# First stage of a two-block model on one core: order of the loads, statistics by stream, place of the scale products

## The chip, the core and the metric

The kernel runs on one core of a Trainium2 chip. The metric is the device time of one execution in microseconds. The core has five engines that run side by side, each with its own queue of instructions: TensorE (PE, matrix products; PEld is its weight load), VectorE (DVE), ScalarE (ACT), GpSimd (POOL) and SyncE (SP, which here only issues transfers). Transfers run on 16 DMA engines.

## The reference, cut to what matters

Two transformer blocks in a row, for 256 tokens of width 1024. The change lies in the start of the first one, where the input x and a context ctx (256 tokens each) are normalised, scaled and shifted by vectors that come from a conditioning vector, and multiplied by the input weights of an mLSTM:

```python
mod = silu(c) @ w_mod + b_mod                 # 6 vectors of 1024: sh1, sc1, ga1, ...
mod_c = silu(c_ctx) @ w_mod + b_mod
hc = rmsnorm(ctx, g_mix) * (1 + csc1) + csh1  # the context stream
hx = rmsnorm(x, g_mix) * (1 + sc1) + sh1      # the latent stream
p = h @ w_in        # q, k, v, o and 16 gates of each token, for hx and hc
```

All that follows (the scan over chunks, the feed-forward parts, the second block) is unchanged.

## The kernel before, in words

The function `start` (lines 492 to 603) makes u = normalised input times scale plus shift for both streams, feature tile by feature tile (8 tiles f of 128 features), and at once multiplies it by the key and gate weights.

- **Loads.** SP issues, in the order of the trace: ccol (both conditioning vectors as columns), the identity, ctx in two pieces `xc` of 512 KB, x in two pieces of 512 KB, `wsc0` (the scale weights of tile 0, 512 KB, line 148), `cols` (all small column vectors, 211 KB), `wsh` of tile 0 (the shift weights, 512 KB, line 552), the key weights of tiles 0 to 3 (`raw`, 320 KB each, line 182), then scale and shift weights of tiles 1 to 4. POOL issues four loads at its start that are needed much later: `mpos` (128 KB, line 664), `row` (the head gain, 512 KB as a broadcast, line 400), `gout` (128 KB, line 1020) and `perm` (64 KB, line 1173).
- **Conditioning rows.** `cond_rows` (line 482) spreads the two conditioning vectors over all partitions with products against the identity.
- **Statistics.** For each of the four 128-token pieces, ScalarE sums the squares of the first 512 features (`mean_square`, line 324) and VectorE those of the other 512 (line 504). When all four are there, one series of ten small VectorE operations (line 507 and `rsqrt_half`, lines 298 to 317) gives the four reciprocal roots `r4`.
- **Features.** `features(h)` (line 510) scales half h of the features of both streams (`xn`, line 517 on VectorE, line 521 on ScalarE), transposes them on TensorE (line 528) and copies them to `xt` (line 530).
- **Vectors.** `vectors(f)` (line 545) makes the scale column of tile f by 8 products of `wsc` with the conditioning columns (`pg`, line 556; each is two hardware instructions, so 16 of them, with two columns each), read from PSUM by VectorE as `gsc` (line 563); and the shift column `shc` by two row sums of `wsh` on VectorE (`ttr`, line 256, 128x1024 each, and line 566). It also loads the key weights and splits them into a high part (a cast on ScalarE, line 236) and a low part (VectorE, line 237). All `pg` share one PSUM buffer (tag "tr" of a pool with one buffer).
- **Keys.** `keys(f)` (line 568) makes u on ScalarE (line 572), for tile 0 also a copy `u0` for wide products (line 576), splits u into high and low (`hilo`, lines 245 and 246), and issues 5 groups j of products into 5 PSUM buffers: per group of tiles 1 to 7 six products of 256 columns (lines 587 to 592), in tile 0 one of 512 columns (line 585) and four of 256.

The text of the program calls vectors(0), vectors(1), keys(0), features(1), and then vectors(f+1) and keys(f) in turn. That is not yet the order on an engine: a planner orders the instructions before the run, by priority (the order of the text; inside `urgent` they count as earlier), by when they are ready according to its own table of costs, and by free buffers. Each engine then works through its list strictly in order. `behind(op, first)` (line 187) adds an order between two instructions of an engine that the planner has to keep; it makes no wait. In `vectors`, for f from 3 on, the first scale product is put behind the key products of tile f-3 (line 558).

The functions that the change touches, as they stand:

Of the kernel before, what the change touches and what calls it, by code (L numbers as in the profile page):

```python
# [7 lines left out]
F32 = mybir.dt.float32  # L8
# [102 lines left out]
def kernel(ctx: ExitStack, tc: tile.TileContext, a: dict, out: bass.AP):  # L111
# [30 lines left out]
    wsc0 = hi_p.tile([128, 1024], F32, name="wsc", tag="w")  # L142
    xc = ar.tile([128, 2, D], F32, name="xc", tag="A")
# [4 lines left out]
    nc.sync.dma_start(out=wsc0, in_=a["w_sc"][0])  # L148

# [30 lines left out]
    def raw_load(src):  # L180
        r = raw_p.tile([128, 1024], F32, name="raw", tag="raw")
        nc.sync.dma_start(out=r[:, :src.shape[-1]], in_=src)
        return r
# [43 lines left out]
    def unit(src, slot=None):  # L227
        n = src.shape[-1]
        r = raw_load(src)
# [12 lines left out]
        return hi, lo  # L242
# [155 lines left out]
    def row_load(src):  # L398
        r = row_p.tile([128, D], F32, name="row", tag="row")
        G.dma_start(out=r[:, :src.shape[-1]], in_=src.partition_broadcast(128))  # L400
        return r
# [90 lines left out]
    def start():  # L492
# [4 lines left out]
        ss = sm.tile([128, 2, 4], F32, name="ss4", tag="ss4", bufs=1)  # L497
        cond_rows()
        for i, src in ((0, xc), (1, x)):
            for t in range(2):  # L500
                j = i * 2 + t
                mean_square(src[:, t, 0:512], ss[:, 0, j:j + 1], D)
                junk = wk.tile([128, D], BF16, name="gjunk", tag="gjunk", bufs=1)
                V.tensor_tensor_reduce(out=junk[:, 0:512], in0=src[:, t, 512:1024], in1=src[:, t, 512:1024], scale=0.5 / D,
                                       scalar=0.0, op0=ALU.mult, op1=ALU.add, accum_out=ss[:, 1, j:j + 1])
# [4 lines left out]
        def features(h):  # L510

            for i, src in ((0, xc), (1, x)):
                xn = wk.tile([128, 2, 512], F32, name="xn", tag="xn")
                for t in range(2):
                    w, r = src[:, t, h * 512:h * 512 + 512], r4[:, i * 2 + t:i * 2 + t + 1]
                    if t == 0:
                        o = V.tensor_scalar_mul(out=xn[:, t, :], in0=w, scalar1=r)
                        if h == 0:
                            mark["xn"] = mark["xn0"] = o
                    else:  # L520
                        o = S.activation(out=xn[:, t, :], in_=w, func=AF.Copy, scale=r)
                        if h == 0:
                            mark["xa"] = o
                for t in range(2):
                    pt = (acc_ps(i, t) if h == 0 else mm_ps() if t == 0 else
                          ps_tr.tile([128, 512], F32, name="pt", tag="tc")).rearrange("p (k n) -> p k n", k=4)
                    for k in range(4):
                        T.transpose(pt[:, k, :], xn[:, t, k * 128:k * 128 + 128], ident)
                    dst = xt[i][:, h * 4:h * 4 + 4, t * 128:t * 128 + 128]
                    (S.copy if t else V.tensor_copy)(dst, pt)  # L530

        with urgent():
            features(0)
# [6 lines left out]
        def kg_unit(f):  # L540
            if f < 1:
                pin(1, 4)
            kgu[f] = unit(a["a_kg"][f])

        def vectors(f):

            wsc = wsc0
            if f:
                wsc = hi_p.tile([128, 1024], F32, name="wsc", tag="w")
                nc.sync.dma_start(out=wsc, in_=a["w_sc"][f])  # L550
            wsh = lo_p.tile([128, 1024], F32, name="wsh", tag="w")
            nc.sync.dma_start(out=wsh, in_=a["w_sh"][f])
            kg_unit(f)
            pg = ps_tr.tile([128, 2], F32, name="pg", tag="tr")
            for k in range(8):
                o = T.matmul(pg, lhsT=wsc[:, k * 128:k * 128 + 128], rhs=ccol[:, k, :], start=(k == 0), stop=(k == 7))  # L556
                if k == 0 and f >= 3:
                    behind(o, mark["kg"][f - 3])
# [4 lines left out]
            o = V.tensor_scalar(out=gsc[:, f, :], in0=pg, scalar1=b1[:, f:f + 1], scalar2=col("g_mix", f, 1),  # L563
                                op0=ALU.add, op1=ALU.mult)
            behind(o, mark["xn"])
            V.tensor_scalar(out=shc[:, f, :], in0=shc[:, f, :], scalar1=col("b_mod", f, 1), scalar2=None, op0=ALU.add)

        def keys(f):
# [11 lines left out]
            hi, lo = kgu[f]  # L580
            for j in range(5):
                s = slice(j * 128, j * 128 + 128)
                p_ = kp[j] if j < 4 else gp
                if f == 0:
                    T.matmul(p_, lhsT=hi[:, s], rhs=u0, start=True, stop=False)
                else:
                    T.matmul(p_[:, 0:256], lhsT=hi[:, s], rhs=uc_hi[:, f, :], start=False, stop=False)
                    T.matmul(p_[:, 256:512], lhsT=hi[:, s], rhs=u_hi[:, f, :], start=False, stop=False)
# [4 lines left out]
            mark.setdefault("kg", []).append(o)  # L593

        vectors(0)
        vectors(1)
        for f in range(8):
            if 0 < f < 7:
                vectors(f + 1)
            keys(f)  # L600
            if f == 0:
                features(1)
# [4 lines left out]
    def mlstm():  # L607
# [56 lines left out]
        G.dma_start(out=mpos, in_=a["mpos"])  # L664
# [23 lines left out]
        gain = row_load(a["a_gain"])  # L688
# [320 lines left out]
    def gla():  # L1009
# [10 lines left out]
        G.dma_start(out=gout, in_=a["gl_gout"].partition_broadcast(128))  # L1020
# [132 lines left out]
    def rope_tables():  # L1153
# [19 lines left out]
        G.dma_start(out=mla.perm, in_=a["perm"])  # L1173
# [329 lines left out]
```

## Time and profile before

| | us |
|---|---|
| median of 3 runs | 1437.48 |
| the runs | 1437.48, 1437.93, 1434.57 |
| profiled execution, its own time | 1434.38 |
| its span | 1432.6 |
| TensorE busy in the span | 1380.0 (96%) |
| VectorE, ScalarE busy | 1113.9 (78%), 720.5 (50%) |
| mean share of the DMA engines' rate | 238 GB/s |

The span runs from the first to the last instruction of the profiled execution, the execution's own time is a little longer, and all rows below count microseconds from the start of the span. An engine that is busy most of the time over 1400 us says little on a stage of 70 us; for that, the views by windows, the chain of waits and the timelines are read. Matrix products are pipelined: the length of one in a row is longer than the distance between two starts, and the distance is what a product costs in a stream.

### The profile page before, as it was taken

What the parts mean: (1) busy time and instruction counts of PE and PEld (TensorE: products, weight loads), DVE (VectorE), ACT (ScalarE), POOL (GpSimd) and SP (SyncE); (2) the same over time, 40 slices, a digit from 0 to 9 for tenths busy, and PEclk for the clock granted to TensorE, in tenths of its full rate; (3) what the DMA queues carried; (4) which work ended last, traced back from release to release, by engine and by line L of the source; (5) the groups of instructions that cost most, each with busy time, mean ns of one, the idle gap of its engine ahead of it and who ended that gap; (6) DMA issues with size and microseconds to landing.
All of it is one profiled execution on the core that took longest, in us unless ns stands there. A gap on an engine that the chain in (4) does not pass through costs nothing.

```text
span 1432.6 us, 22526 instructions
## 1 busy us (share of the span) xinstructions
PE 1380.0 (96%) x8425; PEld 1204.0 (84%) x8425; DVE 1113.9 (78%) x2115; ACT 720.5 (50%) x1188; POOL 18.2 (1%) x42
## 2 busy tenths in 40 slices
PE   6999999999989999999999999999999999899997
PEld 6978877899978999878678999879999776789996
DVE  6887788898688888689788888698878786756563
ACT  4634764545354545566454545554554666644451
POOL 1000000000000000000000000000000000000000
PEclk8999999999999999999999999999999999999999
DMA  8576446797528999568548999469889472366750
GB/s 330 203 265 234 162 151 234 264 323 272 184 96 290 336 340 345 196 222 290 187 154 289 341 335 344 147 202 334 317 310 333 138 253 80 121 198 205 276 170 30
DMA packets 94943, 340.24 MB, mean 238 GB/s; under 512 B 10928, under 2 KB 11248, under 8 KB 94832
## 3 DMA queue, kind: packets, MB, share of 16 engines
q1 hardware_dynamic: 92736, 332.47, 65.6%
q0 software_dynamic: 2096, 6.33, 1.5%
q8 instruction: 66, 1.08, 0.3%
q14 instruction: 45, 0.37, 0.1%
HBM read 337.67 MB, written 1.08 MB: 236 GB/s over the span
## 4 chain that ended last, share of the span: by engine, by line
PE 70%; DVE 11%; DMA 10%; ACT 4%; issue 3%; SPq 0%; DVEq 0%; ACTq 0%; POOLq 0%
PE mm L250 12%; PE mm L252 11%; PE mm L251 11%; PE acc L252 8%; PE acc L250 8%; PE acc L251 8%; DMA raw<-in_cond_w_dram 3%; DVE wlo L237 3%; DVE gjunk L256 2%; PE acc L733 2%; ACT whi L236 1%; ACT ajunk L324 1%; PE pt L347 1%; PE pg L556 1%; DMA row<-d 1%
## 5 line engine op out<-in xcount | busy, mean ns | idle before, releaser
L237 DVE TENSOR_TENSOR wlo<-raw,whi 128x1024 fp32r<-128x1024 f32 (+1 forms) x385 | 462.5, 1207 | 109.6 <-ACT whi L236 106.7
L236 ACT CAST whi<-raw 128x1024 fp32r<-128x1024 f32 (+1 forms) x385 | 395.7, 1038 | 277.1 <-PE mm L251 79.5
L250 PE MATMUL mm<-u_hi,whi 128*128 128x256 f32 x1384 | 388.5, 281 | 0.2 <-DVE hf L831 0.2
L251 PE MATMUL mm<-u_lo,whi 128*128 128x256 f32 x1384 | 386.6, 279 | 0.0
L252 PE MATMUL mm<-u_hi,wlo 128*128 128x256 f32 x1384 | 386.5, 279 | 0.0
L250 PEld LDWEIGHTS mm<-u_hi,whi 128*128 128x128 f32 x1384 | 260.0, 188 | 4.4 <-DVE hf L831 0.6
L251 PEld LDWEIGHTS mm<-u_lo,whi 128*128 128x128 f32 x1384 | 259.3, 187 | 3.3
L252 PEld LDWEIGHTS mm<-u_hi,wlo 128*128 128x128 f32 x1384 | 260.1, 188 | 0.0
L256 DVE CUSTOM_DVE_ANT_0 gjunk<-raw,c 128x1024 bf16<-128x1024 f32 x192 | 234.3, 1221 | 24.1 <-DMA raw<-in_cond_w_dram 16.5
L250 PE MATMUL acc<-whi,hh 128*128 128x512 f32 x388 | 153.6, 398 | 4.5 <-ACT hh L245 4.5
L252 PE MATMUL acc<-whi,hl 128*128 128x512 f32 x388 | 153.3, 397 | 0.3 <-DVE hl L246 0.3
L251 PE MATMUL acc<-wlo,hh 128*128 128x512 f32 x388 | 152.5, 393 | 0.5 <-DVE wlo L237 0.5
L252 PEld LDWEIGHTS acc<-whi,hl 128*128 128x128 f32 x388 | 73.4, 189 | 17.4 <-DVE hl L246 0.7
L250 PEld LDWEIGHTS acc<-whi,hh 128*128 128x128 f32 x388 | 72.9, 188 | 17.5 <-ACT hh L245 5.0
L252 PE MATMUL acc<-whi,u_lo 128*128 128x512 f32 (+1 forms) x216 | 86.7, 403 | 0.5 <-DVE u_lo L246 0.5
L250 PE MATMUL acc<-whi,u_hi 128*128 128x512 f32 (+1 forms) x216 | 86.5, 401 | 0.0
L251 PE MATMUL acc<-wlo,u_hi 128*128 128x512 f32 (+1 forms) x216 | 86.4, 400 | 0.0
L251 PEld LDWEIGHTS acc<-wlo,hh 128*128 128x128 f32 x388 | 73.2, 189 | 14.2 <-DVE wlo L237 1.3
L251 PE MATMUL mm<-wlo,u_hi 128*128 128x512 f32 x144 | 57.3, 398 | 0.0
L250 PE MATMUL mm<-whi,u_hi 128*128 128x512 f32 x144 | 57.2, 397 | 0.0
L252 PE MATMUL mm<-whi,u_lo 128*128 128x512 f32 x144 | 57.0, 397 | 0.0
L946 ACT ACTIVATE sg<-mm 128x256 f32<-128x256 f32 x64 | 24.3, 380 | 59.6 <-PE mm L252 59.5
(734 smaller groups left out, 1998.6 us busy)
## 6 DMA issues: line engine op xcount, KB each, us to landing
raw<-in_cond_w_dram SPq DMA_DIRECT2D x144, 512.0 KB, 5.2
raw<-in_gu_ws_dram SPq DMA_DIRECT2D x128, 512.0 KB, 5.0
raw<-in_dn_dram SPq DMA_DIRECT2D x88, 512.0 KB, 4.9
raw<-in_gu_dram SPq DMA_DIRECT2D x48, 512.0 KB, 4.3
raw<-in_w_mod_dram SPq DMA_DIRECT2D x32, 512.0 KB, 4.3
raw<-in_f_down_dram SPq DMA_DIRECT2D x22, 512.0 KB, 4.6
raw<-in_f_gate_dram SPq DMA_DIRECT2D x18, 512.0 KB, 4.9
raw<-in_a_vo_dram SPq DMA_DIRECT2D x16, 512.0 KB, 5.1
```

Source lines behind the costliest of these rows:

```text
L236: o1 = S.copy(hi[:, :n], r[:, :n])
L237: o2 = V.tensor_tensor(out=lo[:, :n], in0=r[:, :n], in1=hi[:, :n].bitcast(F32), op=ALU.subtract)
L250: T.matmul(ps, lhsT=lh, rhs=rh, start=first, stop=False)
L251: T.matmul(ps, lhsT=lh, rhs=rl, start=False, stop=False)
L252: T.matmul(ps, lhsT=ll, rhs=rh, start=False, stop=last)
L256: return V.tensor_tensor_reduce(out=junk, in0=r, in1=vec, scale=1.0, scalar=0.0, op0=ALU.mult, op1=ALU.add, accum_out=dst)
L324: mark["ms"] = S.activation(out=junk[:, :src.shape[-1]], in_=src, func=AF.Square, scale=float(2 * width) ** -0.5, accum_out=dst)
L347: T.transpose(pt[:, k, :], src[:, (h * 4 + k) * 128:(h * 4 + k + 1) * 128], ident)
L556: o = T.matmul(pg, lhsT=wsc[:, k * 128:k * 128 + 128], rhs=ccol[:, k, :], start=(k == 0), stop=(k == 7))
L733: T.matmul(np_[:, 0:257], lhsT=w[:, d, s, :], rhs=vt[s][:, h, :], start=(i == 0), stop=(i == len(tiles) - 1))
L946: S.activation(out=sg, in_=ps[:, 0:256], func=AF.Silu)
```

## The change

What it does, part by part:

- `wsh0`, the shift weights of tile 0, is loaded right behind `wsc0`, ahead of `cols`.
- The other loads of the stage (key weights of tile 0, then scale, shift and key weights of tile 1, of tile 2 and so on) are issued by SP in one fixed order, each behind the one before (`load`).
- The four loads of POOL are issued by SP, behind the last of these (`late`).
- The statistics and roots are made for each stream by itself (`stats`), in the order ctx statistics, ctx features, x statistics, x features. Of x's first piece, ScalarE sums both halves; VectorE's sum of x's second piece is put behind the scaling of ctx.
- The scale products of tiles 0 and 1 stay in front. Those of tiles 2 to 7 are issued inside `keys(f)` for tile f+2: two products (four hardware instructions) behind each of the groups j = 0 to 3, and the first product of the next group is put behind them. `vectors(f+2)` is now called before `keys(f)`, where `vectors(f+1)` was.

Its core (left out: the loops around `features`, which now takes one stream, and two call sites of `late`):

```diff
+    wsh0 = lo_p.tile([128, 1024], F32, name="wsh", tag="w")
...
     nc.sync.dma_start(out=wsc0, in_=a["w_sc"][0])
+    nc.sync.dma_start(out=wsh0, in_=a["w_sh"][0])
...
+    def late(out, in_):
+        behind(nc.sync.dma_start(out=out, in_=in_), mark["loads"])
...
-        for i, src in ((0, xc), (1, x)):
+        def stats(i, src):
             for t in range(2):
                 j = i * 2 + t
                 mean_square(src[:, t, 0:512], ss[:, 0, j:j + 1], D)
+                if j == 2:
+                    mean_square(src[:, t, 512:1024], ss[:, 1, j:j + 1], D)
+                    continue
...
+                if i:
+                    behind(o, mark["xn0"])
+            js = slice(i * 2, i * 2 + 2)
+            V.scalar_tensor_tensor(out=ss[:, 0, js], in0=ss[:, 0, js], scalar=0.5 * EPS, in1=ss[:, 1, js], op0=ALU.add, op1=ALU.add)
+            r2.append(rsqrt_half(ss[:, 0, js], 2))
...
         with urgent():
-            V.scalar_tensor_tensor(out=ss[:, 0, :], in0=ss[:, 0, :], scalar=0.5 * EPS, in1=ss[:, 1, :], op0=ALU.add, op1=ALU.add)
-            r4 = rsqrt_half(ss[:, 0, :], 4)
...
+            for st in streams:
+                stats(*st)
+                features(0, *st)
...
+        def scales(f, k, after=None):
+            if k == 0:
+                pgs[f] = ps_tr.tile([128, 2], F32, name="pg", tag="tr")
+            pg = pgs[f]
+            o = T.matmul(pg, lhsT=wscs[f][:, k * 128:k * 128 + 128], rhs=ccol[:, k, :], start=(k == 0), stop=(k == 7))
+            mm = o
+            if after is not None:
+                behind(o, after)
+            if k == 7:
+                o = V.tensor_scalar(out=gsc[:, f, :], in0=pg, ...)
+                behind(o, mark["xn"])
+            return mm
+
+        def load(out, in_):
+            o = nc.sync.dma_start(out=out, in_=in_)
+            if "loads" in mark:
+                behind(o, mark["loads"])
+            mark["loads"] = o
...
             hi, lo = kgu[f]
+            turn = None
             for j in range(5):
...
+                if turn is not None:
+                    behind(o, turn)
...
                 o = T.matmul(p_[:, 256:512], lhsT=lo[:, s], rhs=u_hi[:, f, :], start=False, stop=f == 7)
-            mark.setdefault("kg", []).append(o)
+                if j < 4 and f < 6:
+                    for k in (j * 2, j * 2 + 1):
+                        turn = scales(f + 2, k, o)
...
-        vectors(0)
-        vectors(1)
+        for f in range(2):
+            vectors(f)
+            for k in range(8):
+                scales(f, k)
         for f in range(8):
-            if 0 < f < 7:
-                vectors(f + 1)
+            if f < 6:
+                vectors(f + 2)
             keys(f)
...
-        G.dma_start(out=mpos, in_=a["mpos"])
+        late(out=mpos, in_=a["mpos"])
```

## Rows read from the trace of the kernel before

**Rows 1.** Windows, 10 us long: busy time by engine, TensorE clock, DMA share, GB/s

```profile
40.00:50.00 10.00, 10.00 (x90) 10.00 (x88) 7.63 (x16) 3.91 (x9) 0.00 (x0) 1.00 0.58 204
```

**Rows 2.** Chain of waits, 0 to 110 us: start, length, what

```profile
3.85 10.56 DMA wsc<-in_w_sc_dram
...
14.55 3.55 PE pg L556 x16
...
18.10 3.28 PE acc L528 x16
...
21.41 0.59 ACT xt L530
...
23.71 1.09 ACT u L572 x2
...
25.67 0.79 PE acc L585
...
49.20 1.68 PE pg L556 x16
...
50.88 0.23 PE acc L587
...
52.73 1.01 PE pg L556 x10
...
53.74 0.22 PE acc L590
...
68.53 0.13 PE mm L592
```

**Rows 3.** DMA queues, 0 to 16 us: packets, MB, share of 16 engines' time

```profile
q1 hardware_dynamic: 1449, 3.80, 61.2%
...
q0 software_dynamic: 272, 0.85, 24.1%
```

**Rows 4.** Timeline of the SP queue: start, time to issue

```profile
5.54 6.66 SPq L182 DMA_DIRECT2D raw<-in_a_kg_dram  x4
...
13.14 0.33 SPq L550 DMA_DIRECT2D wsc<-in_w_sc_dram  x1
```

**Rows 5.** Timeline of VectorE and ScalarE, 8 to 24 us: start, length

```profile
8.78 0.63 ACT L324 ACTIVATE ajunk<-xc 128x512 bf16<-128x512 f32 x1 [2.04 <-DMA xc<-in_ctx_dram]
...
13.21 0.63 ACT L324 ACTIVATE ajunk<-x 128x512 bf16<-128x512 f32 x1 [0.55 <-DMA x<-in_x_dram]
...
14.08 0.17 DVE L507 SCALAR_TENSOR_TENSOR ss<-ss 128x4 f32<-128x4 f32 x1
...
16.66 0.48 DVE L517 TENSOR_SCALAR xn<-x,r 128x512 f32<-128x512 f32 x1
...
23.39 0.22 DVE L566 TENSOR_SCALAR shc<-shc,cols 128x2 f32<-128x2 f32 x1
```

**Rows 6.** Timeline of TensorE: start, length

```profile
31.78 0.60 PE L528 MATMUL mm<-ident,xn 128*128 128x128 f32 x4
...
53.80 0.28 PE L591 MATMUL acc<-v,wlo 128*128 128x256 f32 x1
...
55.33 0.28 PE L592 MATMUL mm<-u_hi,wlo 128*128 128x256 f32 x1
```

**Rows 7.** Windows before and in the first key products (columns as in rows 1)

```profile
21.50:23.50 2.00, 2.00 (x20) 1.96 (x18) 2.00 (x5) 2.00 (x4) 0.00 (x0) 1.00 1.03 410
...
28.00:31.00 3.00, 3.00 (x14) 2.81 (x14) 3.00 (x6) 0.62 (x2) 0.00 (x0) 0.50 1.01 385
```

**Rows 8.** Groups by shape, 0 to 75 us: busy, mean ns, idle before

```profile
L256 DVE CUSTOM_DVE_ANT_0 gjunk<-wsh,cc 128x1024 bf16<-128x1024 f32 x8 | 9.8, 1220 | 0.0
...
L237 DVE TENSOR_TENSOR wlo<-raw,whi 128x640 fp32r<-128x640 f32 x8 | 6.6, 821 | 0.0
...
L246 DVE TENSOR_TENSOR v<-u,v 128x256 fp32r<-128x256 f32 x8 | 3.4, 422 | 0.0
...
L563 DVE TENSOR_SCALAR gsc<-pg,b,cols 128x2 f32<-128x2 f32 x8 | 2.2, 277 | 6.5 <-PE pg L556 6.4
```

More of the change, by code (lines that the diff above doesn't have):

```diff
@@ L177, with raw_load @@
     mod2 = const.tile([128, 20, 8], F32, name="mod2")
-    def raw_load(src):
+    def raw_load(src, load=nc.sync.dma_start):
         r = raw_p.tile([128, 1024], F32, name="raw", tag="raw")
-        nc.sync.dma_start(out=r[:, :src.shape[-1]], in_=src)
+        load(out=r[:, :src.shape[-1]], in_=src)
         return r
@@ L506, in start @@
-        with urgent():
-            V.scalar_tensor_tensor(out=ss[:, 0, :], in0=ss[:, 0, :], scalar=0.5 * EPS, in1=ss[:, 1, :], op0=ALU.add, op1=ALU.add)
-            r4 = rsqrt_half(ss[:, 0, :], 4)
[L510 to L530, printed above, removed]
@@ L532, in start @@
-        with urgent():
-            features(0)
+                o = V.tensor_tensor_reduce(out=junk[:, 0:512], in0=src[:, t, 512:1024], in1=src[:, t, 512:1024],
+                                           scale=0.5 / D, scalar=0.0, op0=ALU.mult, op1=ALU.add, accum_out=ss[:, 1, j:j + 1])
+                if i:
+                    behind(o, mark["xn0"])
+            js = slice(i * 2, i * 2 + 2)
+            V.scalar_tensor_tensor(out=ss[:, 0, js], in0=ss[:, 0, js], scalar=0.5 * EPS, in1=ss[:, 1, js], op0=ALU.add, op1=ALU.add)
@@ new lines, in stats, with features @@
+            r2.append(rsqrt_half(ss[:, 0, js], 2))
+        def features(h, i, src):
+            xn = wk.tile([128, 2, 512], F32, name="xn", tag="xn")
+            for t in range(2):
+                w, r = src[:, t, h * 512:h * 512 + 512], r2[i][:, t:t + 1]
+                if t == 0:
+                    o = V.tensor_scalar_mul(out=xn[:, t, :], in0=w, scalar1=r)
+                    if h == 0:
+                        mark["xn"] = mark["xn0"] = o
+                else:
+                    o = S.activation(out=xn[:, t, :], in_=w, func=AF.Copy, scale=r)
+                    if h == 0:
+                        mark["xa"] = o
+            for t in range(2):
+                pt = (acc_ps(i, t) if h == 0 else mm_ps() if t == 0 else
+                      ps_tr.tile([128, 512], F32, name="pt", tag="tc")).rearrange("p (k n) -> p k n", k=4)
+                for k in range(4):
+                    T.transpose(pt[:, k, :], xn[:, t, k * 128:k * 128 + 128], ident)
+                dst = xt[i][:, h * 4:h * 4 + 4, t * 128:t * 128 + 128]
+                (S.copy if t else V.tensor_copy)(dst, pt)
@@ L538, in start, with vectors @@
         kgu = {}
-        def kg_unit(f):
+        wscs, pgs = {}, {}
+        def scales(f, k, after=None):
[7 more added lines that the diff above has]
+            if k == 7:
+                o = V.tensor_scalar(out=gsc[:, f, :], in0=pg, scalar1=b1[:, f:f + 1], scalar2=col("g_mix", f, 1),
+                                    op0=ALU.add, op1=ALU.mult)
+                behind(o, mark["xn"])
[5 more added lines that the diff above has]
+            mark["loads"] = o
+        def vectors(f):
+            wsc, wsh = wsc0, wsh0
+            if f:
+                wsc = hi_p.tile([128, 1024], F32, name="wsc", tag="w")
+                load(wsc, a["w_sc"][f])
+                wsh = lo_p.tile([128, 1024], F32, name="wsh", tag="w")
+                load(wsh, a["w_sh"][f])
             if f < 1:
                 pin(1, 4)
[L543 to L558, printed above, removed]
+            kgu[f] = unit(a["a_kg"][f], load=load)
             o = ttr(wsh, cc, shc[:, f, 0:1])
@@ L562, in vectors @@
             ttr(wsh, c1, shc[:, f, 1:2])
-            o = V.tensor_scalar(out=gsc[:, f, :], in0=pg, scalar1=b1[:, f:f + 1], scalar2=col("g_mix", f, 1),
-                                op0=ALU.add, op1=ALU.mult)
-            behind(o, mark["xn"])
+            wscs[f] = wsc
             V.tensor_scalar(out=shc[:, f, :], in0=shc[:, f, :], scalar1=col("b_mod", f, 1), scalar2=None, op0=ALU.add)
@@ L1019, in gla @@
         gout = hp.tile([128, 256], F32, name="gout", tag="gout", bufs=1)
-        G.dma_start(out=gout, in_=a["gl_gout"].partition_broadcast(128))
+        late(out=gout, in_=a["gl_gout"].partition_broadcast(128))
         units, got = {}, {}
@@ L1172, in rope_tables @@
         mla.perm = const.tile([128, 128], F32, name="perm")
-        G.dma_start(out=mla.perm, in_=a["perm"])
+        late(out=mla.perm, in_=a["perm"])
     def rope(src, dst, tokens, rp):
```

22 lines of the change are left out of this document (12 added, 10 removed).

## The prediction, made before the change was run

> **What bounds the kernel now.** The change touches the first stage only, so I read that stage, not the shares of the whole span. First the windows: what is to be seen is where TensorE has idle time and where its clock is full. From 40 to 50 us it is busy all the time at the full clock, while VectorE is busy for 7.6 and ScalarE for 3.9 of 10 us and DMA is at 0.58 [rows 1]. So once the key products run, TensorE's own work sets the pace, and waits of other engines there cost nothing. Second the chain of waits: its first link is the transfer of wsc0, which ends at 14.4; then come the scale products of tiles 0 and 1, transposes, the scaled features u at 23.71, the first key product at 25.67 and the last key product at 68.53 [rows 2]. So the stage has two parts: a front of 25.7 us that hangs on transfers and on a serial chain, and 42.9 us of TensorE's work. Time can be won by a shorter front, or by less work or fewer pauses behind it.
>
> **The loads.** Removed from the front are four transfers that POOL issued. In the first 16 us its queue moved 0.85 MB and took 24.1% of the time of the 16 DMA engines, 3.9 us; the other queue moved 3.80 MB in 61.2% of it, 9.8 us, by whose rate those bytes would take 2.2 us [rows 3]. These are the bounds for how much earlier x and wsc0 land; I take the middle, 3.1 us. The four transfers move to SP, behind the last key weights. They cost SP four issues of about 0.33 us each [rows 4], and the DMA engines 2.2 to 3.9 us around 45 us, where they are at 0.58 [rows 1]; what is queued behind them on SP are the query weights, which nobody waits for until the key products end. POOL loses four issues and had nothing waiting behind them. I cost all that at nothing; if the cover were gone, it would be those 2.2 to 3.9 us. The key weights of tiles 1 to 3 were issued at 5.5 to 12.2 us, ahead of the scale weights of tile 1 at 13.14 [rows 4]; now they alternate by tile. The bytes are the same. Tile 2's scale weights are now needed between the first key products; up to and with them, 5.7 MB are to be moved (the inputs and weights of 0.2 to 0.5 MB each in their new order), at 410 GB/s [rows 7] 13.8 us. Counted from 3.85, where wsc0 is issued [rows 2], that is 17.7, and at most a microsecond to land: ahead of 20.8 us, where I shall put the first key product. wsh0 moves in front of cols, 0.2 MB or 0.5 us; VectorE takes it up only behind x, so that is worth nothing by itself.
>
> **The statistics.** Before, the last piece of x is summed at 13.21, the joint series of small operations begins at 14.08 and x is scaled at 16.66 [rows 5]. The change adds a second series of ten small operations: from 14.08 to about 16.3, 2.2 us of VectorE. The first series (ctx) can run while x is landing: ctx's last piece was summed at 8.78 [rows 5], now 1 to 2 us earlier, so with 0.8 for the sum and 2.4 for the series ctx is scaled from about 10.5 to 11.0. x lands at 13.2 less 3.1, 10.1, but the VectorE half of its second piece now waits for the scaling of ctx: and behind it on that engine stands x's own series: sum from 11.0 to 11.8, series to 14.1, x scaled then, 2.6 us earlier than now. Moving one half of the first piece to ScalarE costs that engine 0.8 us while it waits for x: nothing.
>
> **To the first key product.** TensorE's work in between is 16 hardware products of the scale of tile 0, 3.55 us [rows 2] at half clock, and 16 transposes behind them, 3.28 us [rows 2]. Both ran one after the other; now they start at 11.0 with ctx's transposes, and 6.9 us of work end at 17.8. Then come the copy to xt (0.6), u (1.1) and the 0.87 from the end of u to the first product [rows 2], which gives 20.3, or 21.0 with one weight cast ahead of them. VectorE's side: from x scaled at 14.6 the two sums of wsh0 (2.6), a copy (0.7), a split (0.8), gsc and shc (0.5) [rows 5, 8] make 19.2, and with u and the rest 21.1. I take 20.8 for the first key product against 25.67: **4.9 us earlier**. The bounds are 22.5 to 23.5 (only the transfers shift, by 2.2 to 3.1) and 19.0 (sums slip into the gaps of the small series, transposes at the full clock): 2.2 to 6.7.
>
> **The scale products.** They are moved, not removed: 16 hardware products for each of tiles 2 to 7, 96 in all. Whether spreading them pays can be read from the trace, since the planner had already split one tile's. A block of 16 with the wide product behind it takes 1.68 and 0.23, less 0.118 for a wide one (13 of them from 53.80 to 55.33 [rows 6]): 1.79, or 0.112 each. A group of 10 takes 1.01 and 0.22, less 0.118: 1.11, or 0.111 each [rows 2]. So a split group costs what a block costs, and the edit is worth 0. The Trainium skill (TensorE: Matmul & The Clock Gate, Step-by-step: what each phase is for) says that TensorE pulls the next weight load ahead of a running product; by that, each of the four groups would hide one load more than the one block does, an estimated 3 x 0.112 x 6, 2.0 us less. The split group of 10 in this trace does not show it.
>
> VectorE waited 6.4 us for scale products [rows 8]; those waits go, but TensorE had no pause there [rows 1], so I count 0. What the change adds is order: the next group's first product follows each pair, so that a tile can no longer start with the products whose operands are ready; and one PSUM bank serves all scale products, so the first pair of a tile waits until VectorE has read the last tile's result (gsc). Between them lie 12 wide products, 1.4 us. What VectorE may have to finish first is between 0.3 (gsc alone) and 4.4 us (two sums, a split, two halves of u, gsc [rows 8]); so each of five tile changes costs between 0 and 3.0 us. VectorE's work per tile, 4.6 us, is less than TensorE's, 30 x 0.118 + 1.8 = 5.3, and gsc is due one whole tile ahead, so I take 0, the end that the pause-free rows are nearer to [rows 1].
>
> **The sum.** 4.9 us from the front, 0 behind it. The profiled run took 1434.4 us around a span of 1432.6; that gives 1429.5. The median of the three runs, 1437.5, stands 3.1 above it, one run beside it: by the median it would be 1432.6. I forecast **1431.0**, between the two.
>
> **The rivals.** *The clock stays up* (0.14, faster). The first 25 key products run from 25.67 [rows 2] to 31.78 [rows 6] and their clock is 0.50 [rows 7]; at the full clock 20 narrow ones at 0.118 and 5 of twice the columns at twice that would take 3.5: 2.6 us less. Just before, at 21.5 to 23.5, the clock was full [rows 7], and it fell in the pause in front of u. With TensorE at work from 11 us on it may be full when they start: 1431.0 - 2.6 = 1428.4. Against it: the scale products from 14.55 on took 3.55 us, 0.222 each where 0.112 is the full clock's price, so work of this kind had not raised it by 18 us. The Trainium skill (same page, What's actually happening) says that the clock is low by default and that sustained work releases it; by that rule this rival would be likelier than I make it.
>
> *The lead is lost* (0.22, within the bound). The strict order makes TensorE wait for the late halves of u in the first two tiles, while VectorE still has two tiles' sums in front of it. For it: VectorE gets tile 0's sums only at 14 us and has 4.6 us a tile. Against it: the slack of 0.7 us a tile. Price: 1 to 5 us; 1432 to 1436. That the order doesn't come out as written, since a planner places instructions, belongs here.
>
> *Slower* (0.08). The single PSUM bank: if VectorE's queue holds two sums and a split in front of gsc at each tile change, TensorE stands 5 times 3.0 us, 15 us, in place of a lead of 4.9: 1441. It decides from 1.0 us per tile (lead gone) and makes the kernel over 0.3% slower from 1.9. Against it: sums are spread between other work in VectorE's timeline, and the wait would have to come every time.
>
> *The loads don't land earlier* (0.04): if the queues only share the engines otherwise and x still lands at 13, the regrouping alone remains, about 1 us: 1435.
>
> **How the numbers follow.** About 0.3%, 4.3 us, is what a measurement of this kernel tells from no change. My forecast (0.52) lies at 4.9 between 2.2 and 6.7; about three quarters of it lie beyond 4.3 and count as faster, 0.39; with the clock's 0.14 that makes 0.53. Same: the other quarter, 0.13, the lost lead and the loads, together 0.39. Slower: 0.08. The range reaches from the front's upper bound with the clock, 1434.4 - 6.7 - 2.6, 1425, to 1437.5, where nothing is kept.
>
> **What would show it.** In the changed profile: x's sum at about 10 to 11 us in place of 13.2; the first key product at 19 to 22.5; the last at 62 to 65 in place of 68.5; no idle TensorE between; all pairs at 0.11 a product. It is wrong if TensorE shows pauses released by gsc or the halves of u, if x still lands at 13, or if the last key product is early and the end is not, which would mean that later transfers or VectorE give the lead back.

## The result, and the profile after

The changed kernel is **slower**: median 1444.59 us of 7 runs (1442.02 to 1452.67) against 1436.2 us of 7 runs of the kernel before (1432.32 to 1438.75); the ratio is 1.0069, 95% interval 1.0050 to 1.0088. The profiled execution took 1442.02 us with a span of 1439.8, 7.2 more than before. In the profiled executions all of it arises in the first 115 us:

| progress in the profiled executions, us | before | after | difference |
|---|---|---|---|
| x scaled | 16.66 | 14.23 | -2.4 |
| first key product | 25.67 | 22.77 | -2.9 |
| last key product | 68.37 | 72.66 | +4.3 |
| first value product | 68.49 | 77.95 | +9.5 |
| first score product of the attention | 102.16 | 113.81 | +11.6 |
| end of the span | 1432.6 | 1439.8 | +7.2 |

Some 4 us of the 11.6 come back near 1230 us, where the kernel before has a pause of 2.4 us and a clock of 0.66 over 10 us and the changed one has neither.

The front is as the change wanted it. The next fence is TensorE's timeline (start, length, then in brackets the idle time before and what ended it), with the last key product, the first value product and the first score product.

```profile
11.97 1.85 PE L563 MATMUL pg<-ccol,wsc 128*128 128x2 f32 x16
...
18.59 3.57 PE L563 MATMUL pg<-ccol,wsc 128*128 128x2 f32 x16 [1.23 <-DVE gsc L568]
22.02 1.09 PE L541 MATMUL pt<-ident,xn 128*128 128x128 f32 x4
22.77 0.78 PE L616 MATMUL acc<-u,whi 128*128 128x512 f32 x1
24.41 0.58 PE L623 MATMUL acc<-v,whi 128*128 128x256 f32 x1 [0.86 <-DVE v L248]
26.76 0.58 PE L624 MATMUL acc<-u_lo,whi 128*128 128x256 f32 x1 [1.76 <-DVE u_lo L248]
...
72.66 0.28 PE L626 MATMUL mm<-u_hi,wlo 128*128 128x256 f32 x1
77.95 1.22 PE L252 MATMUL acc<-whi,v 128*128 128x512 f32 x2 [5.01 <-ACT whi L238]
...
113.81 0.38 PE L745 MATMUL mm<-qT,kT 128*128 128x128 f32 x2
```

The scale products of tile 0 start at 11.97 in place of 14.55 [rows 2] and run at the full clock. But the block of tile 1, which before ran at the full clock while u was still being made, now waits 1.23 us for the scale of tile 0, takes 3.57 us at half clock and delays the first key product. Then tile 0 pauses twice for the late halves of u, 0.86 and 1.76 us. The largest pause is new and comes after the stage: 5.01 us in front of the first value product, ended by a ScalarE split of its weights. In the kernel before, the value products follow the last key product without a pause (its timeline of TensorE):

```profile
68.37 0.28 PE L592 MATMUL mm<-u_hi,wlo 128*128 128x256 f32 x1
68.49 0.63 PE L250 MATMUL acc<-whi,v 128*128 128x512 f32 x2
```

The windows show the clock (length, TensorE's busy time and count, granted clock, DMA share, GB/s), first of the kernel before, then of the changed one.

```profile
10.00:55.00 45.00, 38.32 (x280) 0.85 0.81 314
```

```profile
10.00:55.00 45.00, 39.36 (x250) 0.73 0.66 243
```

TensorE is busy a little longer in the changed kernel and gets 30 instructions less done. With two levels, 1.00 and 0.50, a mean of 0.85 over 45 us is 45 x 0.15 x 2 = 13.5 us at half clock, 0.73 is 24.3. The DMA share shows a second thing: 243 in place of 314 GB/s. The steady part answers to [rows 1]:

```profile
40.00:50.00 10.00, 10.00 (x89) 10.00 (x89) 7.19 (x17) 2.33 (x5) 0.00 (x0) 1.00 0.50 167
```

TensorE has no pause there, as before, and takes 5.32 us a tile (the first pairs of three tiles start at 39.02, 44.34 and 49.66). What falls behind is seen on SP. First its timeline (start, time to issue), then its waits (line, what it waited for: total, times, longest).

```profile
18.75 0.42 SPq L575 DMA_DIRECT2D raw<-in_a_kg_dram  x1
34.84 0.33 SPq L575 DMA_DIRECT2D wsc<-in_w_sc_dram  x1
...
50.52 11.80 SPq L184 DMA_DIRECT2D raw<-in_a_q_dram  x4
67.57 5.54 SPq L184 DMA_DIRECT2D raw<-in_a_vo_dram  x4
```

```profile
SPq L575 <- PE pg L563: 24.2, 3, 14.8
...
SPq L184 <- DVE shc L596: 15.7, 3, 5.3
```

SP stands still from 19.2 to 34.84 at the sixth scale weights, whose buffer is held until the scale products of tile 2 end; all later weights stand behind it in the chain. The value weights are issued at 67.57; in the kernel before the same row reads:

```profile
57.72 8.72 SPq L182 DMA_DIRECT2D raw<-in_a_vo_dram  x4
```

So there were two suspects: the pairs with their edges in the first tiles (+4.3 at the last key product, half clock), and the loads (the pause of 5.01).

### The profile page after: what moved, and what is told of

It reads as the page before. It is cut to its first block, busy times and chain, and to the rows that moved or that the text cites. A ratio compares the mean times of both kernels' runs of the same rounds, so it can differ in the third digit from the quotient of the medians.

```text
span 1439.8 us, 22535 instructions
## 1 busy us (share of the span) xinstructions
PE 1386.7 (96%) x8425; PEld 1207.3 (84%) x8425; DVE 1116.2 (78%) x2124; ACT 722.4 (50%) x1190; POOL 16.1 (1%) x38
## 4 chain that ended last, share of the span: by engine, by line
PE 68%; DVE 13%; DMA 9%; ACT 6%; issue 3%; SPq 0%; DVEq 0%; ACTq 0%
PE mm L252 12%; PE mm L254 11%; PE mm L253 11%; PE acc L254 9%; PE acc L252 8%; PE acc L253 8%; DVE wlo L239 3%; DVE gjunk L258 3%; DMA raw<-in_cond_w_dram 2%; PE acc L772 2%; ACT whi L238 2%; ACT ajunk L326 2%; DMA raw<-in_gu_ws_dram 1%; PE pt L349 1%; DMA raw<-in_f_val_dram 1%
## 5 line engine op out<-in xcount | busy, mean ns | idle before, releaser
L238 ACT CAST whi<-raw 128x1024 fp32r<-128x1024 f32 (+1 forms) x385 | 396.2, 1038 | 269.3 <-PE mm L253 77.9
L985 ACT ACTIVATE sg<-mm 128x256 f32<-128x256 f32 x64 | 24.3, 380 | 52.4 <-PE mm L254 52.4
```

The lines of the kernel that those rows point to most:

```text
L985: S.activation(out=sg, in_=ps[:, 0:256], func=AF.Silu)
```

## The experiments

Sixteen kernels ran, each in five rounds beside the kernel before on the same chip; ratios are to that. The fourth set ran on another chip than the first three, so differences between it and them are given by the ratios too.

**First set: the changed kernel less one part.** *Without the edges*:

```diff
-                if turn is not None:
-                    behind(o, turn)
...
-                        turn = scales(f + 2, k, o)
+                        turn = scales(f + 2, k)
```

> The changed kernel without the order edges: neither a group of key products stands behind a pair of scale products nor a pair behind its group; loads, statistics and the two tiles' lead stay. Theory A (the edges make TensorE wait in the first two tiles for the late halves of u, 4.2 us by 39 us): keys of tile 0 done by 32 to 33 us instead of 36, last key product at 68 to 70 us instead of 72.7, the pauses on the halves of u in tile 0 under 0.5 us. The pause behind the stage (theory B, loads) stays at 3 to 5 us if it comes from the loads alone; then the whole is 1439 to 1442 us. Rival (the edges cost nothing, the loads all of it): last key product stays above 72 us and the time at 1443 to 1446.

Measured: 1444.75 us, ratio 1.0076 (1.0055 to 1.0097). The last key product ended at 70.2 in place of 72.9, the pauses in tile 0 were gone, and the time was the same: the pause behind the stage stayed at 5.0. In front of the chain's pause the edges cost 2.7 us at the last key product, and nothing in the end.

*Scale products in blocks again, one tile ahead* (`block` is `vectors` and the eight products of its tile; the pairs in `keys` go, with their edges and the second tile of lead; loads and statistics of the change stay):

```diff
-            if f < 6:
-                vectors(f + 2)
+            if 0 < f < 7:
+                block(f + 1)
```

> The changed kernel with the scale products as before: one block of eight for a tile, one tile ahead; loads and statistics of the change stay. Theory A and B together: as the run without edges within 1.5 us (1438 to 1442), last key product at 68 to 70 us, pause behind the stage still 3 to 5 us, since the loads still stand in one chain. Rival (the spread pairs and the two tiles' lead are the whole loss): faster than the kernel before by the 3 us of the front, 1431 to 1434. Rival (the loads are the whole loss): 1443 to 1446.

Measured: 1444.73, 1.0070 (1.0052 to 1.0088). Without any pair the loss is the same.

*Without the chain*:

```diff
-            if "loads" in mark:
-                behind(o, mark["loads"])
             mark["loads"] = o
```

> The changed kernel without the chain that keeps the stage's loads in one order on SP; the pairs and their edges stay. Theory B (the chain holds the loads of the next stage behind scale weights that wait for a slot): the first weights of the value and output products are issued by 60 us as before instead of 67.6, TensorE's pause at 72.9 to 78 us falls under 1.5 us, the time to 1439 to 1441. The last key product stays at 72 to 73 us by theory A. Rival (the pause follows from the slots alone): pause still 4 to 5 us, time 1443 to 1446.

Measured: 1444.22, 1.0057 (1.0036 to 1.0077). A half hit: the pause behind the stage was gone, as theory B said, but the last key product ended at 77.3, later than with the chain, and the time did not move. TensorE's clock, back at 1.00 from 39.1 to 42.4, fell to 0.50 once more from 42.6 to 49.2, among the pairs of tile 1; in the changed kernel it stayed up there.

*The loads alone, on the kernel before* (order of need, chain, four late loads on SP):

> The kernel before with the loads of the change alone (order of need, one chain, four late loads on SP); statistics and scale products as before. Theory B: first key product at 23 to 25.5 us, last key product 66 to 68.5, but a pause of 3 to 5 us behind the stage: 1435 to 1440, no gain over the kernel before. Rival (the loads cost nothing, all comes from the pairs): no pause above 1 us behind the stage and 1432 to 1435.

Measured: 1444.10, 1.0059 (1.0037 to 1.0080), more than theory B had asked for. The picture is the same: last key product at 72.42, then a pause of 4.99 us, ended by a ScalarE split.

After this set each of two parts looked as if it made the whole loss, and taking one of them away gave nothing.

**Second set: no chain.** *Statistics alone* (blocks, no chain, and the four small loads at the front of POOL's queue again):

```diff
-        late(out=mpos, in_=a["mpos"])
+        G.dma_start(out=mpos, in_=a["mpos"])
```

> The statistics of the change alone, in effect: scale products in blocks, the loads of SP in the order of before (the first shift weights stand one place further on), the four small loads at the front of POOL's queue again. Theory C (the whole loss is the loads': the chain and the four loads on SP push the weights of the next stage's products back): last key product at 66.5 to 69 us, no pause over 1 us behind it, the first attention score product (113.8 us in the changed kernel, 102.2 before) back at 100 to 103, the time 1432 to 1436. Rival (statistics by stream cost the time, by VectorE's order): score product over 108 us and 1440 or more.

Measured: 1435.99, 0.9996 (0.9980 to 1.0012). Theory C holds: what is lost lies in the loads or the pairs, and the statistics alone gain nothing.

*Neither edges nor chain*:

> The changed kernel with neither the order edges of the pairs nor the chain of the loads; the four small loads stay on SP. If the edges (first tile) and the chain (next stage's weights) are the whole loss, each showing only when the other is gone: first score product at 99 to 103 us, time 1430 to 1435. Theory C' (the small loads in SP's queue are a cause of their own, because SP stands still at each until its slot is free): score product at 106 to 113, time 1438 to 1444.

Measured: 1436.18, 1.0005 (0.9980 to 1.0030). Between the two cases: its 12 runs go from 1429.6 to 1444.4, and the profiled execution is the highest of them, with a clock of 0.62 from 10 to 55 us. The clock goes with it: the four runs above 1439 us had a mean granted clock of 0.981 or 0.982 over the whole execution, the eight below 1438 one of 0.986 to 0.991. And the edges, which cost nothing beside the chain, are worth 8.0 us without it (1444.22 against 1436.18, intervals 1.0036 to 1.0077 and 0.9980 to 1.0030).

*Small loads on POOL, held back*, with blocks, no chain and the statistics of the change:

```diff
-        behind(nc.sync.dma_start(out=out, in_=in_), mark["loads"])
+        behind(V.memset(out[:, 0:1] if len(out.shape) == 2 else out[:, 0, 0:1], 0.0), mark["u2"])
+        G.dma_start(out=out, in_=in_)
```

where `mark["u2"]` is VectorE's low half of u of tile 2.

> Statistics of the change, scale products in blocks, SP's loads in the order of before, and the four small loads on POOL but held back until VectorE has split a later tile. It keeps the front's gain (x scaled at 14.2 us instead of 16.7, first key product at 22.5 to 24) without the chain and without loads on SP. Theory C: score product at 99 to 101 us, the time 1431 to 1434, faster than the kernel before by 2 to 3 us. Rival (the front's gain is swallowed by the half clock or by the loads in any order): score product at 102 to 104 and 1435 to 1437.

Measured: 1432.66, 0.9982 (0.9966 to 0.9998).

*The kernel before with the early front and the small loads on SP, no chain*:

> The kernel before with the four small loads on SP and the first shift weights early, but no chain: SP's order is that of before but for the four loads among it. Theory C' (the four loads on SP are a cause of their own): score product at 106 to 112 us, time 1438 to 1443. Rival (the chain alone did it): score product at 100 to 103 and time 1432 to 1436.

Measured: **1429.90, 0.9959 (0.9943 to 0.9974)**: faster than both kernels. Theory C' falls, the rival holds. This run and the loads with their chain (1444.10) differ by the chain alone: it costs 14.2 us. The next three fences are TensorE's timeline, SP's timeline and the window of that run:

```profile
20.91 0.79 PE L596 MATMUL acc<-u,whi 128*128 128x512 f32 x1 [0.19 <-ACT u L587]
```

```profile
51.88 8.72 SPq L184 DMA_DIRECT2D raw<-in_a_vo_dram  x4
```

```profile
10.00:55.00 45.00, 41.99 (x330) 0.92 0.78 298
```

The first key product is 4.8 us earlier than before [rows 2], the value weights 5.8 us, and 0.92 leaves 7.2 us at half clock. TensorE does 330 instructions in a window in which it did 280 before and 250 in the changed kernel.

**Third set: the pairs.** *Neither chain nor pairs* (loads and statistics of the change, blocks):

> The changed kernel without the chain of loads and without the pairs: scale products in blocks one tile ahead, statistics by stream, small loads on SP. Theory D (chain and pairs each cost 10 us or more by themselves, whichever comes first, and statistics cost little): 1429 to 1433 us, first score product at 97 to 101, so that the pairs alone are worth the 11 to 15 us between this run and the run without the chain alone (1444.2). Rival (statistics by stream are dear once the loads are early): 1435 or more, since the same kernel with the statistics of before is at 1429.9.

Measured: 1433.67, 0.9991 (0.9974 to 1.0007), a little above theory D. Against the run without the chain alone (1444.22) the pairs with their edges and the second tile of lead are worth 10.6 us; 8.0 of it went with the edges alone, and the 2.5 that are left (1436.18) lie within the intervals. Against 1429.90 the statistics by stream cost 3.8; with the small loads on POOL it is 1432.66 against 1429.53 (below), 3.1, where the intervals of the ratios overlap. So the rival is right in its direction.

*Pairs alone, on the kernel before* (loads and statistics as before):

> The kernel before with the pairs and the two tiles' lead alone; loads and statistics as before. Theory D: slower than before by 5 to 14 us, 1440 to 1450, with pauses for the late halves of u in the first two tiles and half clock up to 40 us. Rival (pairs cost only where the loads of the change stand beside them): 1434 to 1438.

Measured: 1449.56, 1.0100 (1.0080 to 1.0120); the last key product starts at 81.56, 13.2 us later than before. The new pauses of this stage make only a part of that: 2.69 in tile 1, 0.55 in front of it, 0.6 more in front of the first key product. The rest fits the clock: a mean of 0.62 is 34.2 us at half clock in place of 13.5, and half of the 20.7 more is 10.3. The rows are TensorE's timeline, then two windows:

```profile
42.27 0.58 PE L603 MATMUL acc<-v,whi 128*128 128x256 f32 x1 [2.69 <-DVE v L246]
43.54 0.85 PE L547 MATMUL pg<-ccol,wsc 128*128 128x2 f32 x4
45.67 0.85 PE L547 MATMUL pg<-ccol,wsc 128*128 128x2 f32 x4
...
55.23 0.50 PE L547 MATMUL pg<-ccol,wsc 128*128 128x2 f32 x4
```

```profile
10.00:55.00 45.00, 34.63 (x166) 0.62 0.62 239
...
42.50:54.50 12.00, 12.00 (x56) 0.50 0.21 80
```

From 42.5 to 54.5 TensorE works without a gap, pairs among its key products, and its clock stays at 0.50. The kernel before also starts its key products at half clock, at 25.67 [rows 2, 7], but there they run without pairs and the clock rises (windows of the kernel before):

```profile
25.70:30.70 5.00, 5.00 (x19) 0.50 1.03 400
31.20:35.00 3.80, 3.80 (x35) 1.00 0.65 234
```

*Sums behind the halves* (changed kernel without the chain; `sums(f + 1)` is called in `keys(f)`):

```diff
+        def sums(f):
+            o = ttr(wshs[f], cc, shc[:, f, 0:1])
+            behind(o, mark["xn" if f else "xn0"])
```

> The changed kernel without the chain, pairs and edges kept, and VectorE's two sums over the shift weights of a tile placed behind the late halves of u of the tile before. Theory D1 (the sums in front of the halves are what TensorE waits for between the edges): no pause over 0.5 us for a half of u in tiles 0 and 1, last key product 66 to 71 us instead of 77.3, time 1432 to 1438. Rival D2 (the pairs cost by themselves: TensorE at half clock through the first tiles, and scales that come only with the last pair): pauses smaller, but the last key product stays above 73 us and the time at 1440 or more.

Measured: 1449.54, 1.0122 (1.0088 to 1.0156). D2: no pause over 0.7 us for VectorE's halves of u, and no gain; the last key product ended at 81.0. TensorE now waited 6.1 us in three pauses for ScalarE's half of u, presumably because the sums come later and u needs them.

*The small loads on POOL, held back, statistics of before*:

> The kernel before with the early front (first shift weights ahead, small loads off the front) and nothing else: SP's order otherwise that of before, the four small loads on POOL behind a VectorE instruction of a later tile. If SP's small loads cost anything in their place between the weights, this is faster than the run with them on SP (1429.9): 1426 to 1429. If not, the same within 1 us: 1429 to 1431. Rival (POOL's waiting loads hold up its memsets for the gate chain): over 1431.

Measured: 1429.53, 0.9967 (0.9951 to 0.9983). As on SP within 0.4: where the four small loads are issued doesn't matter once they are off the front.

**Fourth set: where the pairs cost, and which part of the chain.** All four on the kernel of 1429.90. *Pairs in tiles 2 to 5 alone* (`if j < 4 and 2 <= f < 6`, blocks for tiles 2 and 3):

> The kernel before with the early front and the small loads on SP, no chain (1429.9 us), and pairs with their edges in tiles 2 to 5 alone; the scale products of tiles 2 and 3 in blocks. Theory F (pairs are dear only while TensorE's clock is at its lower level, which they prolong): half clock up to 55 us stays at 7 to 14 us in sum, last key product 62 to 66 us, time 1428 to 1432. Rival G (pairs are dear in any tile, since scales come with the last pair): last key product over 70 us, 1438 or more.

Measured: 1438.12, 1.0027 (1.0008 to 1.0046); 12 runs from 1430.4 to 1445.1. Theory F's numbers failed and rival G's came out (1438 or more, last key product over 70: it starts at 74.83). But G's mechanism would show as waits, and TensorE's from 15 to 75 us sum to only 3.0 us. The profiled execution, the highest of the 12, was at full clock before its pairs; a pause of 1.39 us for a half of u came at their beginning, the clock fell, and then:

```profile
33.00:38.00 5.00, 4.64 (x39) 1.00 0.31 110
40.50:56.50 16.00, 16.00 (x76) 0.50 0.60 211
```

Sixteen us without a gap at half clock, as long as pairs stood between the products. In the changed kernel the clock was up when tile 1's pairs ran, and stayed up through all later tiles. So pairs were dear in the tiles in which the clock had fallen, and F had missed that it can fall in any. That executions differ by whether it does was not seen in traces, since one execution is profiled; the mean clocks of the runs, 0.980 in the slowest and 0.988 in the fastest, with exceptions between them, agree.

*Pairs in tiles 0 and 1 alone* (`f < 2`):

> The same base with pairs and edges in tiles 0 and 1 alone, blocks from tile 4 on. Theory F: nearly the whole cost of the pairs: half clock up to 55 us of 24 to 34 us in sum, last key product 72 to 80, time 1440 to 1449. Rival G: a third of the cost, 1432 to 1436.

Measured: 1444.52, 1.0083 (1.0064 to 1.0102): 14.6 us above its base, by the ratios 17.8, no less than the 14.0 of the pairs in six tiles on the kernel before, as theory F has it and against rival G. The pairs in tiles 2 to 5 cost 8.2, by the ratios 9.8, so the two parts don't add up either. *The chain over the first four tiles alone* (`and len(kgu) < 4` at the edge):

> The kernel before with the early front and the chain of loads over the first four tiles alone; the loads behind them are free. Theory B (the chain costs because the later key weights and the next stage's weights stand behind a scale weight that waits for its slot): first value weights issued by 55 us, no pause behind the stage, 1429 to 1433. Rival (the order of the first tiles' loads costs): pause 3 to 5 us or last key product over 70, 1438 or more.

Measured: 1434.87, 1.0002 (0.9989 to 1.0014), between the two theories: the order of the first tiles costs 5.0 us (6.2 by the ratios), and the rest of the chain's 14.2 goes to what it does to the later loads, if the two parts add. In front of the value products stood no pause over 0.5 us.

*Wide products behind the early pairs*, read by nobody:

```diff
                         turn = scales(f + 2, k, o)
+                    extra = ps_tr.tile([128, 512], F32, name="extra", tag="tc")
+                    for _ in range(2):
+                        o = T.matmul(extra, lhsT=hi[:, s], rhs=hi[:, 0:512], start=True, stop=True)
+                        behind(o, turn)
+                        turn = o
```

> As the run with pairs in tiles 0 and 1, with two products of 128x512 behind each of the eight pairs, whose results nobody reads: 16 more products, 3.7 us at full clock by the 0.233 of such a product there, 7 at half. Theory F (what pairs cost is the clock that they hold down, and wide products between them bring it up): the clock is up by 33 us, last key product no later than in the run without the products or earlier, time within 2 us of it or up to 6 less. Rival (no effect on the clock): 4 to 7 us slower than that run.

Measured: 1441.60, 1.0052 (1.0032 to 1.0071): **with sixteen more products the median is 2.9 us lower** than without them, and the last key product starts at 75.01 in place of 77.79. The six runs of each overlap (1436.48 to 1445.67 and 1442.05 to 1448.95), so the gain stands at the edge of the noise; the 4 to 7 us more of the rival are excluded. The windows, without and with the extra products:

```profile
10.00:55.00 45.00, 38.03 (x198) 0.66 0.60 229
```

```profile
10.00:55.00 45.00, 38.15 (x238) 0.81 0.68 250
```

The busy time is the same and 40 more instructions are done, 16 of them the extra ones. The half clock falls from 30.6 to 17.1 us. In tile 0 the clock is back from 32.3 us on, with pairs still to come; without the extra products it stayed at 0.50 to 36.2, beyond the last of them. In tile 1 it doesn't fall at all, where it was 0.50 from 40.0 to 49.8; but the pause in front of that tile is 0.97 us in place of 2.59, and which of the two kept the clock up was not separated. So that the pairs' cost is mostly the clock is supported by two traces and by the mean clocks of the runs; how the share of the edges and of the pairs themselves falls out is not shown.

## Why the prediction was wrong, point by point

**The loads land earlier: right.** VectorE sums x's second piece at 10.43; before, the sum of the same piece on ScalarE began at 13.21 [rows 5]. x is scaled at 14.23, forecast 14.1. In the first 16 us POOL's queue is empty, and SP's moved 5.24 MB in place of 3.80 [rows 3]:

```profile
q1 hardware_dynamic: 1885, 5.24, 84.8%
```

**The fixed order of the loads at no cost: the step that failed first.** I wrote of the regrouped loads that the bytes are the same, and of the small ones that the query weights behind them have time, and costed all of it at nothing. I had counted the issues that SP gains, but not that in a chain each load inherits the wait for a buffer of the one in front. The sixth scale weights wait until 34.84, and the key weights and the next stage's weights with them. They then come one tile at a time; the raw buffers (five) come free only when VectorE has split a tile's key weights, and the chain of waits of the changed kernel shows that split inside a loop of VectorE and ScalarE, once for each tile:

```profile
47.60 1.14 DVE gjunk L258
...
48.85 1.22 DVE gjunk L258
...
50.08 0.74 DVE wlo L239
50.81 0.15 DVE shc L596
...
50.99 1.09 ACT u L602 x2
52.08 0.30 ACT v L247
...
52.41 0.43 DVE v L248
52.83 0.34 DVE u_lo L248
53.17 1.13 DVE gjunk L258
```

Two sums, the split, ScalarE's u and its halves, until the next sums: 5.57 us, a little more than TensorE's 5.32. I had set VectorE's 4.6 us a tile against TensorE's 5.3; in this loop ScalarE's 1.39 stand in series with VectorE's work. So the query weights are issued until 62.3 and the value weights at 67.57, and TensorE stands 5.01 us and goes on at half clock until 83.

The transfer is not what TensorE waits for at the end. The first value weights landed at 70.9, 1.8 us before the last key product started; they wait for their split on ScalarE, which works through its list from 67.7 to 77.9 without a pause. The rows are the issue at 67.57 with its time to landing, then ScalarE's timeline:

```profile
raw<-in_a_vo_dram SPq DMA_DIRECT2D x1, 512.0 KB, 3.3
```

```profile
73.27 0.68 ACT L663 ACTIVATE gb<-mm,cols 64x512 f32<-64x512 f32 x1
73.98 1.04 ACT L238 CAST whi<-raw 128x1024 fp32r<-128x1024 f32 x1
75.04 1.28 ACT L666 ACT_TABLE_LOAD   x1
76.34 0.63 ACT L666 ACTIVATE gb<-gb 64x512 f32<-64x512 f32 x1
76.87 1.03 ACT L238 CAST whi<-raw 128x1024 fp32r<-128x1024 f32 x1
```

The first of these reads the last key products; behind it stand the cast of other weights, a table load and another gate operation, and only then the cast that ends the pause. All four kernels with the whole chain have this series and a pause of 4.99 to 5.01. In the kernel before, three casts in a row from 63.32 on stand ahead of it. That the planner put it behind the gates because it reckoned with late weights is my reading and was not tried. Price: 0 forecast; 14.2 us measured on the kernel with the statistics of before, 11.1 on that of the change (1444.73 against 1433.67).

**The statistics: right in time, of no value.** ctx is scaled at 10.03 (forecast 10.5 to 11.0), x at 14.23. But alone they change nothing (0.9996), and beside the early loads their medians are 3 to 4 us higher, in one of the two pairs within the noise. There the first key product comes at 22.20, against 20.91 without them, and the half clock from 10 to 55 us is 13.5 us against 7.2. That the order on VectorE makes it so (scale of tile 0 behind the second sum, and TensorE waiting for it) is read from the timeline, not tried.

**First key product at 20.8: 22.77.** The term left out is tile 1's block of scale products: it stood behind the transposes before [rows 2], in the shadow of u; now the wide copy of u is ready at 20.6, and the block with 1.23 of waiting and 3.57 at half clock holds the first key product up. In the run without edges the same block ran at the full clock, 1.95 us, and the first key product came at 21.09: most of the miss is the clock. The front's gain was 2.9 of 4.9. That 4.9 can be had, without the statistics and without the chain, the run of 1429.90 shows: 4.8.

**Scale products at the same price: right as a price, wrong as a cost.** A group of six products and a pair takes 40.18 - 39.02 = 1.16 us in the changed kernel's tile 1 at full clock, 6 x 0.118 and 4 x 0.112 make 1.156. The gain by the weight loads pulled ahead does not show here either. But I priced the pairs at full clock and asked only what waits they bring. What I left out is the clock that had fallen and, with pairs between the key products, stayed down: 14.0 us for the pairs and edges alone, some 10 of it clock by the estimate above. I had the rows for the question, since the products of the scale, run alone from 14.55, stayed at half clock; I used them against the rival in which the clock stays up, and not against the change.

**The order edges at no cost: wrong**, by 2.6 us of pauses in tile 0 (0.86 and 1.76), the mechanism of the rival "the lead is lost", within its price of 1 to 5. In the end the edges cost nothing beside the chain (run without edges) and 8.0 us without it, so they are the larger part of what the pairs cost there, above the rival's price. The PSUM bank, my slower case, shows one wait of 1.23 us and none at the later tile changes.

**Why the parts don't add.** Chain and pairs each cost 10.6 to 14.6 us alone and no more together (1444.59 against 1433.67 without either, 10.9). The first value product shows how: it needs the last key product and its split weights. With the chain it starts between 75.22 and 78.4 in four kernels, with pairs or without, since the split is late; with the pairs and no chain at 77.12, since the keys are. The first score product comes between 112.3 and 115.7 in all five, and at 103.33 with neither. Each part hides behind the other, and so taking away one gave nothing; this is read from one execution of each. The result lies outside my range and beyond every rival, because no case of mine had the chain in it, or a clock that stays down.

## What to carry to other kernels

A fixed order on a load queue makes each transfer wait for the buffers of all in front of it: before fixing it, list for each load what frees its buffer and when, and what the next stage's loads behind it would lose. When an engine then stands, compare the landing of its operand with the end of the operation that prepares it: here the weights were there, and the engine that splits them was busy with other things. When two edits that each cost something end at the same meeting point, undoing one shows nothing: undo both, then add them one by one to a clean base. Work that is free at the full clock is to be priced again for the stretch where the clock is low, and asked whether it lets the clock rise.

## What the runs showed of the hardware

TensorE worked 12 and 16 us without a gap at a clock of 0.50, when two-column products stood between its key products; in the kernel before, key products alone had gone from 0.50 to 1.00 between 30.7 and 31.2. Once at 1.00, the clock was not lowered by the same pairs (changed kernel, 39 to 72 us, no pause over 0.55); behind a pause of 1.25 us (run without the chain) and of 1.39 (pairs in tiles 2 to 5) it fell while they ran. The Trainium skill (TensorE: Matmul & The Clock Gate, What's actually happening) says that the low clock is the default and that activity releases it; the runs agree for the key products, and show besides that work without a gap, with such pairs in it, did not do so here. With 16 more products of 128x512 that nobody reads the mean clock from 10 to 55 us was 0.81 in place of 0.66 (one execution each), and the median time 2.9 us lower, at the edge of the noise.
